# Stick-breaking attention: one hand-ordered pipeline over all head pairs, with each block's totals carried in one row of the next block

## The chip, the cores and the metric

The kernel runs on one core of one Trainium2 chip, as one program. The metric is the device time in microseconds (us) of one execution; the figure compared is the median over several executions. All durations in this document come from a profiled execution of the kernel or from its measured times.

## The reference

One layer of a hybrid decoder trunk, on 1024 positions of width 1024, in float32. `h` is the normalised input, and one wide projection gives the queries, keys and values of 8 heads of 64 columns, three conv operands and two gates:

```python
h = rms_norm(x, norm_mix_pre)
q, k, v, cb, cc, cx, g_att, g_conv = split(h @ w_in)
# per head and block of 128 queries, strictly causal (s < t):
z = q @ k.T / sqrt(64)
log_keep = where(strict, log_sigmoid(-z), 0)
later = reverse_cumsum(log_keep, axis=keys) - log_keep
w = where(strict, exp(log_sigmoid(z) + later), 0)
o = w @ v
y_att  = o @ w_att_branch
y_conv = (cb * causal_dwconv3(cc * cx)) @ w_conv_branch
m = sigmoid(g_att) * y_att + sigmoid(g_conv) * y_conv
x = x + rms_norm(m @ w_out, norm_mix_post)
h = rms_norm(x, norm_ffn_pre)
a, g = split(causal_dwconv3(h @ w_up))
x = x + rms_norm((gelu(g) * a) @ w_down, norm_ffn_post)
```

What matters here is `later`: for each query, the sum of softplus(z) = -log_keep over all keys that lie between a key and the query. A weight is exp(z - A), where A is the sum of softplus(z) over this key and all later ones.

## The kernel before

Every float32 operand of a large product is kept as two float16 parts, a high one (written by ScalarE, `AF.Copy`) and a low one (the rest, written by VectorE), and each product is three matrix passes (high-high, high-low, low-high; `PASSES`, `split` L84 to L87). A weight tile of 128x1024 is loaded, its sum of squares is taken on ScalarE (`sumsq`, L56), a one-column matmul and three small VectorE instructions give a power-of-two scale (`scale_of`, L74 to L79), and `split` makes the two halves. `wseq` is the order in which the weights are loaded, `prep` (and below it `wfetch`, `wsplit`) keeps a few of them ahead.

The layer runs in stages: the norm of x and its transposes with the v projection (in a hand order), the **attention stage** in `mixer`, then the branches, gates and output projection, then the feed-forward part.

The attention stage works on four head pairs `j`. For a pair the keys are cut into blocks `i` of 128 and the queries into halves `c` of 512. A **unit** is one key block against one query half, for both heads: keys on the 128 partitions, queries along the free dimension, so a tile is 128 x 2 x up to 512. Key blocks are taken from the last to the first; those on the diagonal have fewer queries (128, 256, 384 or 512). There are 12 units in a pair and 48 in all; 24 of them are 2x512 wide, and 8 each are 2x384, 2x256 and 2x128 wide. `attention(j)` writes each unit in four steps:

- `stage1`: scores into PSUM tile `z` (6 matmuls with 64 rows of weights, through `mm`, L600); VectorE scales them, bounds them at 44 and masks the diagonal block, into `zc` (L615 with a mask tile, L618 without); ScalarE takes exp and then ln(1 + .), giving `sp` = softplus (L622, L623); the halves of `sp` go into `sh` (L625 ScalarE, L626 VectorE).
- `stage2`: four matmuls with the triangle `tri[:, 0]` add, for each key, the sum over this and the later keys of the block into PSUM tile `A`, which lives for all units of a query half; VectorE forms `zc - A` (L638), ScalarE takes exp (L640), and the halves of the weights go into `w` (L642 ScalarE, L643 VectorE).
- `stage2b`: four matmuls more, with the complement of the triangle, `tri[:, 1]`, add the rest of the block's sum, so that every row of `A` holds the block's total when the next block comes:

```python
def stage2b(u):
    if u["i"] > 0:
        for h in range(2):
            for hl in range(2):
                mm(acc["A"][:, h, off:], self.tri[:, 1, :], sh[:, hl, h, off:], start=False, stop=False)
```

- `stage3`: six matmuls of the weights with `v16` into PSUM tile `o`; after the last block of a half ScalarE and VectorE write `o16` (L668, L669).

Between the units' steps, `merge` puts pieces of other work in proportion: the projections of the other head pairs (`qk_tile`), the v tiles, the conv operands and the gates (each 24 matmuls of 512 columns per half, `cm_half`, L200), and half of the conv branch's product (`branch(0, d, pm)`, L580, evicted by VectorE at L587). These need 3 of the 8 PSUM banks (`pm`); `z` and `A` have two each and `o` has one. The written order is not the final one: a scheduler orders the instructions of PE, DVE and ACT, with raised priority for the units.

SyncE's queue (SP) issues the weight loads in order. GpSimd (POOL) only makes masks at the start and does a few small powers.

Of the kernel before, what the change touches and what calls it, by code (L numbers as in the profile page):

```python
# [24 lines left out]
P = 128  # L25
T = 1024
# [5 lines left out]
EPS = 1e-6  # L32
GROUPS = (2, 4, 4, 4, 4, 4)
# [4 lines left out]
class Layer:  # L38
# [43 lines left out]
    nsc = 0  # L82

# [122 lines left out]
    def build(self):  # L206
# [7 lines left out]
        nt("q", 0), nt("k", 0)  # L214
        for j in range(4):
            if j < 3:
                nt("q", j + 1), nt("k", j + 1)
            nt("cc", j), nt("cx", j), nt("cb", j)
        nt("gc", 0), nt("ga", 0)
# [10 lines left out]
        with ExitStack() as top:  # L230
# [24 lines left out]
            self.tri = c.tile([P, 2, P], F16, tag="tri", name="tri")  # L255
            nc.vector.tensor_copy(self.tri[:, 0, :], tri32)
            nc.vector.tensor_scalar(self.tri[:, 1, :], tri32, -1.0, 1.0, ALU.mult, ALU.add)
# [6 lines left out]
    def mixer(self, mid):  # L264
        tc, nc, a = self.tc, self.nc, self.a
        hT = self.hp.tile([P, 2, KD, T], F16, tag="hT", name="hT")
        with ExitStack() as ph1:
# [12 lines left out]
            def qk_tile(j, which):  # L280
                w, inv = self.prep(f"{which}{j}") if j else self.wdone[f"{which}0"]
# [3 lines left out]
                s = stk[j]  # L285
                for c in range(2):
                    ps = pm.tile([P, NH], F32, tag="pm", name=f"p{which}{j}_{c}")
                    yield from self.cm_half(w[0], hT, ps, c)
                    sl = ds(c * NH, NH)
                    nc.scalar.activation(s[which][:, 0, sl], ps, AF.Copy, scale=2.0 ** -15)  # L290
                    nc.vector.scalar_tensor_tensor(s[which][:, 1, sl], ps, 2.0 ** -15, s[which][:, 0, sl],
                                                   ALU.mult, ALU.subtract)
                if which == "k":
                    cz = self.small(f"cz{j}", keep=True)
                    self.mul(cz[:, 0:1], s["iq"], inv)
                    self.mul(cz[:, 1:2], cz[:, 0:1], cst[:, 0:1])
                    s["cz"] = cz[:, 1:2]
                yield


            with tc.tile_pool(name="ptp", bufs=2, space=bass.MemoryType.PSUM) as ptp:
# [28 lines left out]

                def v_out(tt, pv):
                    pj = pv.rearrange("p (j two d) -> p j two d", two=2, d=64)
                    nc.scalar.activation(v16[tt // 2][:, tt % 2, :, 0:4:3, :], pj, AF.Copy, scale=2.0 ** -15)
                    for e in range(2):
                        nc.vector.scalar_tensor_tensor(v16[tt // 2][:, tt % 2, :, 1 + e, :], pj[:, :, e, :], 2.0 ** -15,
                                                       v16[tt // 2][:, tt % 2, :, 3 * e, :], ALU.mult, ALU.subtract)

                def v_tile(tt):
                    pv = pm.tile([P, NH], F32, tag="pm", name=f"pv{tt}")
# [8 lines left out]
                    v_out(tt, pv)  # L348
# [61 lines left out]
                with tc.manual_schedule(engines={ET.PE, ET.DVE, ET.Activation}):  # L410
# [78 lines left out]
                    gens0 = [qk_tile(0, "q"), qk_tile(0, "k")]  # L489
                    run(gens0[0], 8)  # L490
# [7 lines left out]
                    run(gens0[1], 8)  # L498
                    turn_x(7)
                    high(7)  # L500
                    low(7)

# [10 lines left out]
            def conv_tile(j):  # L513
                sm = self.small(f"cv{j}", keep=True)
                t = {}
                u = self.slot([P, T], F32, f"u{j}")
                for n, which in enumerate(("cc", "cx", "cb")):
                    w, inv = self.prep(f"{which}{j}")
                    self.mul(sm[:, n:n + 1], inv_h, inv)
                    sc = sm[:, n:n + 1]  # L520
                    if which == "cb":
                        pf[j] = self.slot([P, T], F32, f"pf{j}")
                        nc.scalar.activation(pf[j], u, AF.Copy, scale=self.cmw[:, j, 2:3])
                        for lag in (1, 2):
                            nc.vector.scalar_tensor_tensor(pf[j][:, lag:], u[:, :T - lag],
                                                           self.cmw[:, j, 2 - lag:3 - lag],
                                                           pf[j][:, lag:], ALU.mult, ALU.add)
                    for c in range(2):
                        ps = pm.tile([P, NH], F32, tag="pm", name=f"p{which}{j}_{c}")
                        yield from self.cm_half(w[0], hT, ps, c)  # L530
                        sl = ds(c * NH, NH)
                        if which == "cc":
                            nc.scalar.activation(u[:, sl], ps, AF.Copy, scale=sc)
                        elif which == "cx":
                            nc.vector.scalar_tensor_tensor(u[:, sl], ps, sc, u[:, sl], ALU.mult, ALU.mult)
                        else:
                            nc.vector.scalar_tensor_tensor(pf[j][:, sl], ps, sc, pf[j][:, sl],
                                                           ALU.mult, ALU.mult)
                self.sumsq(pf[j], smp_[:, j:j + 1], f"p{j}")
                yield  # L540

            def p_split():
                s_, inv = self.scale_of(smp_, 4, keep=True)
                acts[0] = []
                for j in range(4):
                    t = self.slot([P, 2, T], F16, f"p16_{j}")
                    self.split(t, pf[j], s_, f"p{j}")
                    acts[0].append(t)
                inv_x[0] = inv
                yield  # L550

            sig = {}

            def gate0(which):

                w, inv = self.prep(f"{which}0")
# [3 lines left out]
                for c in range(2):  # L560
                    ps = pm.tile([P, NH], F32, tag="pm", name=f"p{which}0_{c}")
                    yield from self.cm_half(w[0], hT, ps, c)
                    nc.scalar.activation(s[:, ds(c * NH, NH)], ps, AF.Copy, scale=sc)
                sig[which, 0] = s

            def branch(bi, d, pm):

                which = ("wc", "wa")[bi]
                w, inv = self.prep(f"{which}{d // 2}")
# [716 lines left out]
```

## Time and profile before

| what | value |
|---|---|
| time, median of 3 executions | 1369.34 us (1369.21 to 1369.62) |
| span of the profiled execution, first to last instruction | 1365.7 us |
| median less the span: what lies around the span | 3.6 us |
| TensorE (PE) busy | 1336.1 us (98%) |
| VectorE (DVE) busy | 1028.6 us (75%) |
| ScalarE (ACT) busy | 860.7 us (63%) |
| mean granted TensorE clock | 0.998 |

The profiled execution's own time is not listed apart from its span; the times in the table are those of the unprofiled executions. A PE that is busy is not a PE at its peak, since matmuls are pipelined: the mean duration of one 512-column matmul is 379 ns, but in a row they follow one another more closely, and the busy time of a group counts overlapped time once.

The stages in the trace: the v and first q, k halves until about 57 us; the attention stage with the work put between its units from there until 442 us, where the last matmul of `branch(0, 7, pm)` ends; branches, gates and output projection after that; the feed-forward part to the end.

### The profile page before, as it was taken

What the parts mean: (1) busy time and instruction counts of PE and PEld (TensorE: products, weight loads), DVE (VectorE), ACT (ScalarE), POOL (GpSimd) and SP (SyncE); (2) the same over time, 40 slices, a digit from 0 to 9 for tenths busy, and PEclk for the clock granted to TensorE, in tenths of its full rate; (3) what the DMA queues carried; (4) which work ended last, traced back from release to release, by engine and by line L of the source; (5) the groups of instructions that cost most, each with busy time, mean ns of one, the idle gap of its engine ahead of it and who ended that gap; (6) DMA issues with size and microseconds to landing.
All of it is one profiled execution on the core that took longest, in us unless ns stands there. A gap on an engine that the chain in (4) does not pass through costs nothing. (4 is left out here: it accounts for less than half of the span.)

```text
span 1365.7 us, 16990 instructions
## 1 busy us (share of the span) xinstructions
PE 1336.1 (98%) x6651; PEld 607.7 (44%) x6651; DVE 1028.6 (75%) x1610; ACT 860.7 (63%) x1204; POOL 34.2 (3%) x52
## 2 busy tenths in 40 slices
PE   6999999999999999999999999999999999999997
PEld 3444444444444444444454444444444444444443
DVE  6667777777775965878788985984894896699855
ACT  6668778787775775666466577652761673476524
POOL 2000000000000000000010000000000000000002
PEclk9999999999999999999999999999999999999999
DMA  7102111101111121351331123122220321313216
GB/s 264 62 1 62 32 31 32 38 25 39 40 31 47 32 62 31 93 185 36 119 124 62 62 62 123 39 87 85 70 78 16 123 62 62 109 45 124 63 46 109
DMA packets 26576, 96.06 MB, mean 70 GB/s; under 512 B 3072, under 2 KB 3200, under 8 KB 26496
## 3 DMA queue, kind: packets, MB, share of 16 engines
q1 hardware_dynamic: 25056, 89.74, 20.3%
q0 software_dynamic: 1440, 5.24, 2.1%
q8 instruction: 52, 0.85, 0.2%
q14 instruction: 28, 0.23, 0.1%
HBM read 86.58 MB, written 8.39 MB: 70 GB/s over the span
## 5 line engine op out<-in xcount | busy, mean ns | idle before, releaser
L1156 PEld LDWEIGHTS <-wh_u 128*128 128x128 f16 x1848 | 178.8, 98 | 217.3 <-issue 3.5
L1048 PE MATMUL pd<-wdh,f 128*128 128x512 f16 (+1 forms) x1068 | 230.3, 377 | 2.8 <-ACT wdh L86 1.2
L1048 PEld LDWEIGHTS <-f 128*128 128x128 f16 x1068 | 104.4, 98 | 127.2 <-issue 4.3
L86 ACT ACTIVATE wh_u<-ws_u,sc 128x1024 f16<-128x1024 f32 (+1 forms) x66 | 64.7, 998 | 102.9 <-DVE sc L78 79.3
L1055 DVE SCALAR_TENSOR_TENSOR yacc<-pd,sd,yacc 128x512 f32<-128x512 f32 (+1 forms) x81 | 58.5, 740 | 72.7 <-PE pd L1048 65.2
L1156 PEld LDWEIGHTS <-wh_g 128*128 128x128 f16 x588 | 56.9, 98 | 68.7 <-issue 0.4
L859 PE MATMUL py<-wh_wo,m 128*128 128x512 f16 x384 | 83.9, 379 | 0.0
L87 DVE SCALAR_TENSOR_TENSOR wh_u<-ws_u,sc,wh_u 128x1024 f16<-128x1024 f32 (+1 forms) x66 | 72.1, 1099 | 9.5 <-ACT wh_u L86 9.4
L643 DVE SCALAR_TENSOR_TENSOR w<-zc,w 128x1024 f16<-128x1024 f32 (+3 forms) x48 | 45.7, 955 | 34.5 <-ACT w L642 34.4
L622 ACT ACTIVATE sp<-zc 128x1024 f32<-128x1024 f32 (+3 forms) x48 | 40.2, 838 | 46.7 <-DVE zc L615 29.1
L600 PE MATMUL A<-sh,tri 128*128 128x512 f16 (+3 forms) x352 | 67.8, 322 | 0.0
L1233 DVE SCALAR_TENSOR_TENSOR ugu<-cgu,cw_g,ugu 128x1023 f32<-128x1023 f32 (+1 forms) x44 | 56.2, 1278 | 11.3 <-ACT ugu L1231 10.9
L1233 DVE SCALAR_TENSOR_TENSOR ua<-cau,cw_a,ua 128x1023 f32<-128x1023 f32 (+1 forms) x44 | 56.1, 1276 | 1.4 <-ACT ua L1231 1.3
L859 PEld LDWEIGHTS <-m 128*128 128x128 f16 x384 | 37.5, 98 | 44.1
L626 DVE TENSOR_TENSOR sh<-sp,sh 128x1024 f16<-128x1024 f32 (+3 forms) x48 | 45.7, 952 | 12.9 <-ACT sh L625 12.7
L640 ACT ACTIVATE zc<-zc 128x1024 f32<-128x1024 f32 (+3 forms) x48 | 40.0, 834 | 15.4 <-DVE zc L638 15.0
L638 DVE SCALAR_TENSOR_TENSOR zc<-A,zc 128x1024 f32<-128x1024 f32 (+3 forms) x48 | 45.5, 949 | 2.3 <-PE A L600 2.3
L56 ACT ACTIVATE jk_u<-ws_u 128x1024 bf16<-128x1024 f32 x44 | 46.4, 1054 | 0.9
L200 PE MATMUL pk<-hT,wh_k 128*128 128x512 f16 x192 | 46.8, 380 | 0.0
L200 PE MATMUL pq<-hT,wh_q 128*128 128x512 f16 x192 | 44.3, 379 | 1.3 <-DVE sc L79 1.3
L623 ACT ACTIVATE sp<-sp,one 128x1024 f32<-128x1024 f32 (+3 forms) x48 | 44.6, 928 | 0.8
L200 PE MATMUL pcb<-hT,wh_cb 128*128 128x512 f16 x192 | 44.8, 379 | 0.0
(620 smaller groups left out, 2606.4 us busy)
## 6 DMA issues: line engine op xcount, KB each, us to landing
ws_u<-w_up_nt SPq DMA_DIRECT2D x44, 512.0 KB, 3.7
ds<-w_down SPq DMA_DIRECT2D x22, 512.0 KB, 6.1
wd<-w_down SPq DMA_DIRECT2D x22, 512.0 KB, 3.7
ws_g<-w_in_nt SPq DMA_DIRECT2D x14, 512.0 KB, 3.6
x<-x SPq DMA_DIRECT2D x8, 512.0 KB, 8.0
ws_wo<-w_out SPq DMA_DIRECT2D x8, 512.0 KB, 7.1
xr<-x SPq DMA_DIRECT2D x8, 512.0 KB, 4.3
out<-x SPq DMA_DIRECT2D x7, 512.0 KB, 2.9
```

Source lines behind the costliest of these rows:

```text
L56: self.nc.scalar.activation(self.junk(f"jk_{name}"), src, AF.Square, accum_out=acc)
L86: self.nc.scalar.activation(dst[:, 0, :], src, AF.Copy, scale=s)
L87: self.nc.vector.scalar_tensor_tensor(dst[:, 1, :], src, s, dst[:, 0, :], ALU.mult, ALU.subtract)
L200: nc.tensor.matmul(ps, w[:, wi, ds(k * P, P)], hT[:, hi, k, ds(c * NH, NH)], start=n == 0, stop=n == last)
L600: nc.tensor.matmul(out, w, mv, skip_group_check=True, **kw)
L626: nc.vector.tensor_tensor(sh[:, 1, :, off:], sp[:, :, off:], sh[:, 0, :, off:], ALU.subtract)
L643: nc.vector.scalar_tensor_tensor(w[:, 1, :, off:], zc[:, :, off:], 2.0 ** 14, w[:, 0, :, off:], ALU.mult, ALU.subtract)
L859: nc.tensor.matmul(ps, m16[k][:, hi, ds(tt * P, P)], wo[k][:, wi, sl], start=k == 0 and p == 0, stop=k == 7 and p == 2)
L1048: nc.tensor.matmul(pd[nh], f16[g][k][:, hi, ds(tt * P, P)], w[k][:, wi, ds(*part)], start=run is runs[0] and n == 0, stop=run is runs[-1] ...
L1055: nc.vector.scalar_tensor_tensor(y[:, sl], ps, sm[:, 0:1], y[:, sl], ALU.mult, ALU.add)
L1156: nc.tensor.matmul(ps, w[wt][:, wi, ds(wc * NH + k * P, P)], self.block(i, hi, k), start=first and n == 0, stop=n == 3 * KH - 1, skip_grou ...
L1233: nc.vector.scalar_tensor_tensor(u[:, lag:], c[:, :T - lag], sm[:, 2 - lag:3 - lag], u[:, lag:], ALU.mult, ALU.add)
```

## The change

The attention stage is written anew:

- **Totals.** The complement matmuls (`stage2b`) and the second triangle are gone. `A` is a fresh tile for each unit (`sums`). Row 0 of `A` holds the sum over the whole block; `carry` adds this one row, by a VectorE instruction on one partition, to one row of the next block's `sp`. An operand may start at partition 96, so keys 96 and 127 of each block change places (`swap` for k: three small VectorE copies per key half; `swap_v` for v: rows through DRAM, 4 DMAs on SP's queue for each of the four `v16` tiles), and triangle and mask are made to match (small GpSimd instructions at the start).
- **Weights.** They are exp(z) times exp(-A) instead of exp(z - A). ScalarE reads the scores from PSUM itself (`expz`, with the scale as an operand), VectorE bounds e = exp(z) in SBUF at 1.2e19 (`bound`; the 128 diagonal columns with the mask, the others with one constant), ScalarE takes exp(-A) from PSUM (`expa`), VectorE multiplies (`times`).
- **Order.** PE, DVE and ACT run the whole stage in the written order (`manual_schedule`). One loop goes over all 48 units: `sums(k)`, `scores(k+2)`, side matmuls, `carry(k+1)` and so on. The side work on ACT and DVE (evictions, weight splits, conv taps) is queued in `Side` and let out at three places in each turn of the loop (`q.point`), by a budget per engine; a PSUM bank that is wanted and not yet evicted forces its eviction at that place.
- **Side work.** The order of weights is `FILL`, up to four ahead; the second halves of q0 and k0 move behind the start of the attention; the four halves `branch(0, 4..7)` are evicted by ScalarE, the sigmoid of the first gates comes at the end of the stage.

The core of the diff (the queued forms of the conv, gate and weight work are left out, they hold the same instructions as before; so are `p_ops` and `need`):

```diff
+EMAX = 1.2e19
+FILL = ("q0 k0 q1 k1 cc0 cx0 q2 k2 cb0 cc1 cx1 cb1 cc2 cx2 q3 k3 cb2 cc3 cx3 cb3 gc0 ga0").split()
...
-            self.clamp = att.tile([P, 2, NH], F16, tag="clamp", name="clamp")
-            nc.gpsimd.memset(self.clamp, 44.0)
-            nc.gpsimd.affine_select(self.clamp[:, :, :P], self.clamp[:, :, :P], [[0, 2], [1, P]], ALU.is_gt,
-                                    -30000.0, base=0, channel_multiplier=-1)
+            self.mask = att.tile([P, 2, P], F16, tag="mask", name="mask")
+            nc.gpsimd.memset(self.mask, 1.0)
+            nc.gpsimd.affine_select(self.mask, self.mask, [[0, 2], [1, P]], ALU.is_gt, 0.0, base=0,
+                                    channel_multiplier=-1)
+            nc.gpsimd.affine_select(self.mask[96:128, :, 97:], self.mask[96:128, :, 97:], [[0, 2], [0, 31]],
+                                    ALU.is_ge, 1.0, base=30, channel_multiplier=-1)
...
+            def swap_v(i):
+                rows = [dram.tile([1, 2, 4, 4, 64], F16, tag=f"vr{i}_{e}", name=f"vr{i}_{e}") for e in range(2)]
+                for e, r in enumerate((96, 127)):
+                    nc.sync.dma_start(rows[e], v16[i][r:r + 1])
+                for e, r in enumerate((127, 96)):
+                    nc.sync.dma_start(v16[i][r:r + 1], rows[e])
...
+                    kb = x.rearrange("p h (b t) -> p h b t", t=P)[:, :, 4 * c:4 * c + 4]
+                    kt = self.smp.tile([P, 2, 4, 1], F16, tag="kt", name=f"kt{j}{c}", bufs=2)
+                    nc.vector.tensor_copy(kt, kb[:, :, :, 96:97])
+                    nc.vector.tensor_copy(kb[:, :, :, 96:97], kb[:, :, :, 127:128])
+                    nc.vector.tensor_copy(kb[:, :, :, 127:128], kt)
...
+            def expz(u):
+                off = u["off"]
+                e = u["e"] = att.tile([P, 2, NH], F32, tag="e", name=f"e{u['nm']}", bufs=3)
+                nc.scalar.activation(e[:, :, off:], u["z"][:, :, off:], AF.Exp, scale=stk[u["j"]]["cz"])
+
+            def bound(u):
+                off, e = u["off"], u["e"]
+                if u["diag"]:
+                    dg = slice(off, off + P)
+                    nc.vector.scalar_tensor_tensor(e[:, :, dg], e[:, :, dg], EMAX, self.mask, ALU.min, ALU.mult)
+                    off += P
+                if off < NH:
+                    nc.vector.tensor_scalar(e[:, :, off:], e[:, :, off:], EMAX, None, ALU.min)
+
+            def softplus(u):
+                off = u["off"]
+                sp = u["sp"] = att.tile([P, 2, NH], F32, tag="sp", name=f"sp{u['nm']}", bufs=2)
+                nc.scalar.activation(sp[:, :, off:], u["e"][:, :, off:], AF.Ln, bias=self.one)
+
+            def carry(u):
+                if not u["top"]:
+                    A, o0 = acc["A"]
+                    nc.vector.tensor_tensor(u["sp"][96:97, :, o0:], A[0:1, :, o0:], u["sp"][96:97, :, o0:], ALU.add)
...
+            def sums(u):
+                off, sh = u["off"], u["sh"]
+                A = pat.tile([P, 2, NH], F32, tag="A", name=f"A{u['nm']}")
+                acc["A"] = A, off
+                for h in range(2):
+                    for hl in range(2):
+                        mm(A[:, h, off:], self.tri, sh[:, hl, h, off:], start=hl == 0, stop=hl == 1)
+
+            def expa(u):
+                off = u["off"]
+                g = u["g"] = att.tile([P, 2, NH], F32, tag="g", name=f"g{u['nm']}", bufs=1)
+                nc.scalar.activation(g[:, :, off:], acc["A"][0][:, :, off:], AF.Exp, scale=-1.0)
+
+            def times(u):
+                off, e = u["off"], u["e"]
+                nc.vector.tensor_tensor(e[:, :, off:], e[:, :, off:], u["g"][:, :, off:], ALU.mult)
...
-                def stage2b(u):
-                    if u["i"] > 0:
-                        off, sh = u["off"], u["sh"]
-                        for h in range(2):
-                            for hl in range(2):
-                                mm(acc["A"][:, h, off:], self.tri[:, 1, :], sh[:, hl, h, off:],
-                                   start=False, stop=False)
...
+            with tc.manual_schedule(engines={ET.PE, ET.DVE, ET.Activation}):
+                pump()
...
+                base = 18.0
+                for k in range(nu + 1):
+                    n = (est[k] * lam - att_pe[k]) / chunk
+                    at(sums, k)
+                    at(scores, k + 2)
+                    run_to(base + 0.35 * n)
+                    at(carry, k + 1)
+                    at(sp_high, k + 1)
+                    at(expa, k)
+                    if ready:
+                        ready.pop(0)[1]()
+                    q.point(free[k])
+                    at(sp_low, k + 1)
+                    at(expz, k + 2)
+                    at(times, k)
+                    at(bound, k + 2)
+                    at(w_high_, k)
+                    q.point(free[k])
+                    run_to(base + 0.65 * n)
+                    at(softplus, k + 2)
+                    at(w_low_, k)
+                    at(weigh, k - 1)
+                    q.point(free[k])
+                    run_to(base + n)
+                    if ready:
+                        ready[0][0]()
+                    base += n
+                run_to(total)
...
+    def bank(self, name):
+        while len(self.live) >= 3:
+            t = next(t for t in self.first + self.rest if any(o.bank == self.live[0] for o in t.ops))
+            self.late.append((name, self.live[0], len(t.ops)))
+            self.step(t)
+        self.live.append(name)
+        return self.tile(name)
...
+    def point(self, share=1.0):
+        self.clock += 1
+        for e in self.credit:
+            self.credit[e] = min(self.credit[e] + share, self.CAP)
+        for lst in (self.first, self.rest):
+            for t in list(lst):
+                self.advance(t)
+                if not t.ops and t in lst:
+                    lst.remove(t)
```

Of the loop's numbers, `n` is the count of side pieces (three matmuls each, 400 in all) put into turn `k`, `est[k]` a weight that grows with the widths of the units k to k+2, and `lam` scales these weights so that all pieces are used up at the end.

More of the change, by code (lines that the diff above doesn't have):

```diff
@@ L542, in p_split @@
[L542 to L556, printed above, removed]
+            sig = {}
+            wtasks, wpos = {}, [3]
@@ new lines, in mixer @@
+                q.drain("end")
+                for name, t in wtasks.items():
+                    if any(o.eng == "sum" for o in t.ops):
+                        for o in t.ops[:2]:
+                            if o.cost == 1.2:
+                                o.f()
+                        st = next(o.st for o in t.ops if o.st)
+                        self.wraw[name] = st["sm"], [st["t"]]
+                    else:
+                        q.force(t, name)
+                for which in ("gc", "ga"):
+                    nc.scalar.activation(sig[which, 0], sig[which, 0], AF.Sigmoid)
@@ L722, in mixer @@
+            self.fpos = wpos[0]
+            self.wpos = next((i for i, (n_, _) in enumerate(self.wseq) if i >= 3 and n_ not in self.wdone), n_w)
             pha.close()
```

592 lines of the change are left out of this document (413 added, 179 removed).

## The prediction

> **What bounds the kernel now.** First the page's busy times and slices, then a table of stretches, then the waits of PE.
>
> ```profile
> span 1365.7 us, 16990 instructions
> ...
> PE 1336.1 (98%) x6651; PEld 607.7 (44%) x6651; DVE 1028.6 (75%) x1610; ACT 860.7 (63%) x1204; POOL 34.2 (3%) x52
> ...
> PE   6999999999999999999999999999999999999997
> ```
>
> PE is busy in every slice but the first and the last. A busy PE need not be a full one, so the next view is the attention stage by itself, with three other stretches.
>
> ```profile
> core 0: us, PE busy (x) PEld busy (x) DVE busy (x) ACT busy (x) POOL busy (x), PEclk, DMA share, GB/s
> 57.30:442.30 385.00, 383.65 (x2154) 167.56 (x2154) 271.33 (x420) 285.98 (x379) 0.00 (x0) 1.00 0.12 36
> 442.30:475.00 32.70, 31.46 (x148) 14.35 (x148) 32.56 (x39) 25.01 (x37) 0.00 (x0) 1.00 0.11 33
> 700.00:780.00 80.00, 76.65 (x367) 35.76 (x366) 71.44 (x116) 46.13 (x73) 6.23 (x6) 1.00 0.20 66
> 1180.00:1260.00 80.00, 80.00 (x376) 36.28 (x375) 74.48 (x114) 54.36 (x74) 0.00 (x0) 1.00 0.29 102
> ```
>
> The first row is the stage that the change rewrites: 385.0 us, PE busy for 383.65 at full clock, ACT for 286 (74%), DVE for 271 (70%). The waits of PE from 40 to 560 us are these two, and no more:
>
> ```profile
> PE pr L74 <- DVE ywc L587: 1.3, 1, 1.3
> PE pq L200 <- DVE sc L79: 1.3, 1, 1.3
> ```
>
> So this stage is bound by PE's work: no unit's chain and no eviction is late in it. What leaves PE there shortens the stage, as long as ACT and DVE still deliver in time.
>
> **The sum of the change: PE.** What goes is `stage2b`. Each pair has three units of a half c=0 and seven of a half c=1 with i > 0: of these two are 128 columns wide, two 256, two 384 and four 512. With 4 matmuls per unit and 4 pairs that is 32 matmuls each of 128, 256 and 384 columns and 64 of 512. The rows of `A` hold them with the sums, which stay:
>
> ```profile
> L600 PE MATMUL A<-sh,tri 128*128 128x512 f16 x160 | 40.2, 379 | 0.0
> L600 PE MATMUL A<-sh,tri 128*128 128x384 f16 x64 | 13.6, 327 | 0.0
> L600 PE MATMUL A<-sh,tri 128*128 128x256 f16 x64 | 10.5, 274 | 0.0
> L600 PE MATMUL A<-sh,tri 128*128 128x128 f16 x64 | 6.8, 221 | 0.0
> ...
> 382.78 1.89 PE L600 MATMUL A<-sh,tri 128*128 128x512 f16 x8
> ```
>
> The complement's share is 64/160 of 40.2 and half of the other three: 16.1 + 6.8 + 5.25 + 3.4 = 31.5 us. That share counts the lead-in of each group. Eight in a row take 1.89 us (last row), the last one of them 0.379, so the other seven follow at 0.216 us, where the share gives 40.2/160 = 0.251. At that ratio the complement is 27.1 us. I take 29, with 27.1 and 31.5 as ends. Scores, sums, weighted sums, the 400 pieces of side work and the scale totals stay as many on PE as they were.
>
> **DVE.** It loses the scaling with the bound, from PSUM, and gets it back as `bound`; `zc - A` becomes `times`, the same size at the same price; new are `carry`, the swaps of k, and a lost eviction.
>
> ```profile
> L618 DVE TENSOR_SCALAR zc<-z,cz x16: 1271/1283/1285, 111.8 to 388.1; 128x1024 f32<-128x1024 f32 x16
> L615 DVE SCALAR_TENSOR_TENSOR zc<-z,cz,clamp x32: 474/878/1285, 64.5 to 355.9; 128x256 f32<-128x256 f32 x8, 128x512 f32<-128x512 f32 x8, 128x768 f32<-128x768 f32 x8, 128x1024 f32<-128x1024 f32 x8
> ...
> L638 DVE SCALAR_TENSOR_TENSOR zc<-A,zc 128x1024 f32<-128x1024 f32 x24 | 29.2, 1216 | 0.8 <-PE A L600 0.8
> L638 DVE SCALAR_TENSOR_TENSOR zc<-A,zc 128x768 f32<-128x768 f32 x8 | 7.6, 948 | 0.0
> L638 DVE SCALAR_TENSOR_TENSOR zc<-A,zc 128x512 f32<-128x512 f32 x8 | 5.5, 681 | 1.4 <-PE A L600 1.4
> L638 DVE SCALAR_TENSOR_TENSOR zc<-A,zc 128x256 f32<-128x256 f32 x8 | 3.3, 417 | 0.0
> ...
> L78 DVE TENSOR_SCALAR sc<-sc 128x1 int32<-128x1 int32 x26 | 3.8, 150 | 0.4
> ...
> 3.00 0.21 DVE L257 TENSOR_SCALAR tri<-tri 128x128 f16<-128x128 f32 x1
> ...
> L587 DVE TENSOR_SCALAR ywc<-pywc,sgn x8: 743/750/751, 424.5 to 442.7; 128x512 f32<-128x512 f32 x8
> ```
>
> - Removed: 16 x 1.28 + 32 x 0.878 = 48.6 us, and 8 x 0.750 = 6.0 us of branch evictions that go to ACT.
> - `carry`: its width is that of the unit before it, for 40 units: 16 of 1024 elements, 8 each of 768, 512 and 256. No row shows an instruction on one partition. Its ends are that it costs what a one-element instruction does (0.150 us, 6 us in all) and what the same elements cost on 128 partitions, as L638 does from the same PSUM tile: 16 x 1.216 + 8 x (0.948 + 0.681 + 0.417) = 35.8 us. I take 35.8, since in L638's rows the price follows the elements of a partition.
> - `bound`: the diagonal part, 256 elements with a mask, 32 x 0.474 = 15.2 us (L615's smallest). The rest has `carry`'s widths. At L638's rate it is 35.8 us; but L638 grows by (1216 - 417)/768 = 1.04 ns an element, and L257, float32 from SBUF with constants, took 0.21 us for 128, which after 0.150 leaves 0.5 ns. At that rate 1024, 768, 512 and 256 elements are 0.68, 0.55, 0.42 and 0.28 us, 20.9 us in all. I take 20.9, as L257 is the nearer row in kind.
> - Swaps of k: 21 copies at 0.150 is 3.1 us.
>
> DVE: 271.3 - 48.6 - 6.0 + 35.8 + 15.2 + 20.9 + 3.1 = 291.7 us, up to 306.6 with the slower `bound`. [...]
>
> ```profile
> 388.08 1.28 DVE L618 TENSOR_SCALAR zc<-z,cz 128x1024 f32<-128x1024 f32 x1
> 389.27 1.21 DVE L638 SCALAR_TENSOR_TENSOR zc<-A,zc 128x1024 f32<-128x1024 f32 x1
> ```
>
> These two overlap by 0.09 us. If `carry` and the instruction behind it each lose that, DVE has 40 x 0.18 = 7 us more, 314 at the worst. [...]
>
> **ACT.** Still five passes per unit.
>
> ```profile
> L622 ACT ACTIVATE sp<-zc 128x1024 f32<-128x1024 f32 x24 | 25.3, 1054 | 26.3 <-DVE zc L618 17.6 <-DVE zc L615 8.7
> L325 ACT ACTIVATE hT<-pt_pre,g_pre 128x1024 f16<-128x1024 f32 x8 | 8.8, 1106 | 8.0 <-PE pt_pre L322 8.0
> L585 ACT ACTIVATE ywc<-pywc,sgn x8: 667/687/689, 447.0 to 464.5; 128x512 f32<-128x512 f32 x8
> ```
>
> `expz` reads PSUM with a scale operand as L325 does, 0.05 us dearer than L622; over 36 units' worth of full width 1.9 us. The eight evictions from DVE are 5.5 us. ACT: 286.0 + 7.4 = 293.4.
>
> **What hides what.** With 29 us less the stage lasts 356. ACT then has 82% of it, DVE 82% (worst 88%). Two stretches of the feed-forward part, quoted above, show PE with DVE that full: at 93% PE lost nothing in 80 us, at 89% it lost 3.35. Their mean is 1.7 in 80, for 356 us 7.5, with 0 and 15 as ends. I add 7.5.
>
> The new recurrence, `sums` to `carry` to `sp_high` to `sp_low` to the next `sums`, is no bound by itself:
>
> ```profile
> L625 ACT ACTIVATE sh<-sp 128x1024 f16<-128x1024 f32 x24 | 25.0, 1043 | 0.6 <-PE A L600 0.6
> L626 DVE TENSOR_TENSOR sh<-sp,sh 128x1024 f16<-128x1024 f32 x24 | 29.2, 1216 | 1.3 <-ACT sh L625 1.3
> ```
>
> Four matmuls, 3 x 0.216 + 0.379 = 1.03, then 1.22, 1.04 and 1.22 us: 4.5 at full width, where 356/48 = 7.4 us pass per unit on average. But `carry` is a new wait on DVE for PE, and `sp_high` a new one on ACT for DVE; behind the first stand `sp_low`, `times` and the side work of the turn, behind the second `expa`, `expz` and `w_high_`. That is the first rival.
>
> Moves that I cost at nothing: the 16 row DMAs of `swap_v` stand in SP's queue ahead of the weights, which are fetched up to four ahead, with 48 side pieces of 3 x 0.216 = 0.65 us in front of the first that needs one, 31 us:
>
> ```profile
> ws_q<-w_in_nt SPq DMA_DIRECT2D x4, 512.0 KB, 3.9
> ```
>
> A row out and back is two DMAs in turn, by this row's landing 8 us, which the 31 cover; without that cover PE would wait for those 8 once. The masks are made at the start, where GpSimd's mask of 2x512 gets four times smaller. At the stage's start PE's wait at L200 (1.3 us) may go, since v6 comes first; the next that can be late there is the score tile of the first unit, which has 6 side pieces before it. The wait for `ywc` at L74 then is one for ACT. At its end the last unit still has `expa` to `o16`; the branch products in `wc` do not need it. That may cost 0 to 7 us; I take 1.3, and start and end cancel.
>
> Sum: -29 + 7.5 = -21.5 on the profile's span of 1365.7, 1344.2. The median of the runs, 1369.34, lies 3.6 above the span, so **1347.8 us**. This case's own range: -31.5 - 1.3 + 0 is 1336.5, -27.1 + 15 + 7 is 1364.2.
>
> **Rivals.**
>
> *1. In a fixed order ACT stands behind DVE, and DVE behind PE (slower).* In the written turn ACT's `sp_high(k+1)` waits for `sums(k)` and `carry(k+1)`, 1.0 + 1.22 us at full width, and `w_high_(k)` for `times(k)`, 1.22. Before, the scheduler put other work there: ACT's idle time of 385 - 286 = 99 us was free to lie anywhere. Over 24 full units and 24 of about 60%, the first wait is 24 x 2.2 + 24 x 1.3 = 84 us, the second the sum of L638's busy times, 45.6. Where side work of the turn before fills these gaps, nothing is lost; unfilled, ACT needs 293 + 130 = 423 us, and the stage lasts that. It is slower than before from 385 - 293 = 92 of 130 unfilled, 71%. At 80% the stage is 397, +12: 1381 us. For it: ACT and DVE are over 80% full, and side work is let out at three places only. Against: the next rows are two of the five passes over all 48 units.
>
> ```profile
> L622 ACT ACTIVATE sp<-zc 128x1024 f32<-128x1024 f32 (+3 forms) x48 | 40.2, 838 | 46.7 <-DVE zc L615 29.1
> L623 ACT ACTIVATE sp<-sp,one 128x1024 f32<-128x1024 f32 (+3 forms) x48 | 44.6, 928 | 0.8
> ```
>
> Four at 40.2 and one at 44.6 are 205 us, so some 88 of ACT's 293 are side work that can lie in the gaps, and `sums` has 7.4 - 4.5 = 2.9 us of slack in a turn.
>
> *2. The gain goes into evictions (no change).* Three PSUM banks take a half of 24 x 0.216 = 5.2 us each, and an eviction now needs one of the three places in a turn for ACT and the next for DVE, 7.4/3 = 2.5 us apart. Before, PE waited for one once:
>
> ```profile
> PEld L200 <- DVE k L291: 1.1, 1, 1.1
> ```
>
> Of the 400 pieces, eight to a half but for the branch, about 40 halves lie behind others; at 0.6 us each (an estimate: half of that 1.1) 24 us come back, which is 1371.8 us, and 1359.8 if only half of them are late; 1366 in the middle. For it: DVE is also full right after the stage (32.56 of 32.70 us), so nothing can be put off. Against: a bank that is wanted forces its eviction ahead of the rest.
>
> **How the numbers follow.** Forecast 58%, rival 1 24%, rival 2 18%. A measurement here tells about 0.2%, 2.7 us. The forecast's range is faster throughout; of rival 2 I count 10 points faster, 4 the same, 4 slower. Faster 0.68, same 0.04, slower 0.28. The range starts at 1337, the forecast's best end, which leaves out some 5%, and reaches to 1382, in the middle of rival 1, which leaves out some 12%.
>
> **What would show it.** Matmuls into `A` fall from 352 to 192, and the stage, read to the last matmul of `pywc` 7, ends near 421 instead of 442. PE's waits in it are below 15 us in all. `carry` at 1024 elements shows near 1.2 us, `bound` near 0.7. If PE waits on `sp_low`, or on score tiles behind `expz`, for over 30 us, rival 1 holds; if on evictions, rival 2. A `carry` of several us, or ACT over 330 us busy, would prove the sum wrong.

## The result and the profile after

The changed kernel takes 1352.99 us (median of 4) where the kernel before takes 1369.28 us: 16.3 us less, ratio 0.990 with a 95% interval of 0.9879 to 0.992. In a second series the same kernel came to 1354.53 against 1368.38 (0.9908, 0.989 to 0.9926). One execution of the changed kernel in each series took longer (1358.6 us) and is part of these medians and ratios; without it the first series has a median of 1352.85 us, 0.988 of the time before.

The page of the changed kernel, its span, the busy time of PE and PE's slices:

```profile
span 1351.2 us, 16781 instructions
...
PE 1311.1 (97%) x6491; PEld 589.9 (44%) x6491; DVE 1047.4 (78%) x1689; ACT 864.1 (64%) x1213; POOL 34.5 (3%) x58
...
PE   5999999999988999999999999999999999999997
```

PE lost 25 us of work and 160 instructions (192 matmuls into `A` in place of 352), and two slices, the twelfth and thirteenth, are no longer full: they are the end of the attention stage. The table of stretches has the stage up to the last matmul of `branch(0, 7)`, and the time right behind it:

```profile
57.30:425.70 368.40, 358.38 (x1988) 149.44 (x1987) 290.26 (x501) 283.95 (x382) 0.00 (x0) 1.00 0.12 37
425.70:460.00 34.30, 31.30 (x149) 14.10 (x146) 31.61 (x42) 31.21 (x45) 0.00 (x0) 1.00 0.15 46
```

The stage went from 385.0 to 368.4 us, 16.6 less: PE's busy time fell by 25.3, its idle time rose from 1.35 to 10.0. Behind the stage PE waits 3.0 us where it waited 1.3. That is 14.9 in all, and the spans differ by 14.5. The medians differ by 1.8 us more. The 3.6 us that the prediction puts around the span come from a median and the span of one profiled execution; in the later series, which list time and span of each single execution, the two differ by 1.6 to 1.9 us, once by 2.8. So the profiled execution of the kernel before seems to have been a faster one: its 1365.7 us and 1.8 make 1367.5, and the four executions of the kernel before in the first series lie between 1367.49 and 1369.62 us.

The waits of PE from 45 to 455 us:

```profile
PE pywc L1439 <- ACT ywc L765: 2.6, 1, 2.6
PE pr L76 <- DVE rb L73: 2.2, 1, 2.2
PE pr_p L1439 <- DVE rb_p L706: 1.8, 1, 1.8
PE pcc L1439 <- ACT u L664: 1.4, 1, 1.4
PE pga L211 <- ACT sgc L734: 1.3, 1, 1.3
PE pcb L211 <- DVE sc_cb L89: 0.8, 1, 0.8
PE pga L1439 <- ACT sga L734: 0.8, 1, 0.8
PE pywc L760 <- ACT ywc L765: 0.8, 1, 0.8
PE z L785 <- ACT e L804: 0.5, 1, 0.5
PE pcb L1439 <- DVE pf L667: 0.4, 1, 0.4
PE A L785 <- DVE sh L832: 0.2, 1, 0.2
```

Only the rows of `z` and `A`, 0.7 us together, are the attention's own chain. All others wait for side work: an eviction that has to free a PSUM bank (`ywc`, `u`, `sgc`, `sga`, `pf`), or the scale of a weight or of the conv product (`rb`, `rb_p`, `sc_cb`). In us these are 7.3 for evictions and 4.8 for scales.

The new instructions, by form:

```profile
L785 PE MATMUL A<-sh,tri 128*128 128x512 f16 x96 | 24.6, 379 | 0.0
L785 PE MATMUL A<-sh,tri 128*128 128x384 f16 x32 | 6.5, 326 | 0.0
L785 PE MATMUL A<-sh,tri 128*128 128x256 f16 x32 | 5.0, 272 | 0.2 <-DVE sh L832 0.2
L785 PE MATMUL A<-sh,tri 128*128 128x128 f16 x32 | 3.1, 219 | 0.0
...
L823 DVE TENSOR_TENSOR sp<-A,sp 1x1024 f32<-1x1024 f32 x16 | 19.5, 1218 | 8.1 <-PE A L785 7.8
L813 DVE TENSOR_SCALAR e<-e 128x1024 f32<-128x1024 f32 x16 | 11.1, 693 | 5.8 <-ACT e L804 5.6
L810 DVE SCALAR_TENSOR_TENSOR e<-e,mask 128x256 f32<-128x256 f32 x32 | 13.5, 421 | 5.5 <-ACT e L804 5.3
```

`carry` on one partition costs 1.218 us, as much as `zc - A` before on 128 (1.216); `bound` 0.693 us.

### The profile page after: what moved, and what is told of

It reads as the page before. It is cut to its first block, busy times and chain, and to the rows that moved or that the text cites. A ratio compares the mean times of both kernels' runs of the same rounds, so it can differ in the third digit from the quotient of the medians.

```text
span 1351.2 us, 16781 instructions
## 1 busy us (share of the span) xinstructions
PE 1311.1 (97%) x6491; PEld 589.9 (44%) x6491; DVE 1047.4 (78%) x1689; ACT 864.1 (64%) x1213; POOL 34.5 (3%) x58
## 5 line engine op out<-in xcount | busy, mean ns | idle before, releaser
L828 ACT ACTIVATE sh<-sp 128x1024 f16<-128x1024 f32 (+3 forms) x48 | 40.4, 842 | 52.3 <-DVE sp L823 51.9
L823 DVE TENSOR_TENSOR sp<-A,sp 1x1024 f32<-1x1024 f32 (+3 forms) x40 | 35.9, 897 | 26.3 <-PE A L785 21.8
L858 DVE SCALAR_TENSOR_TENSOR w<-e,w 128x1024 f16<-128x1024 f32 (+3 forms) x48 | 45.8, 954 | 10.1 <-ACT w L854 9.9
L854 ACT ACTIVATE w<-e 128x1024 f16<-128x1024 f32 (+3 forms) x48 | 40.4, 843 | 17.4 <-DVE e L849 16.5
L818 ACT ACTIVATE sp<-e,one 128x1024 f32<-128x1024 f32 (+3 forms) x48 | 44.4, 925 | 6.0 <-DVE e L813 3.1
L849 DVE TENSOR_TENSOR e<-e,g 128x1024 f32<-128x1024 f32 (+3 forms) x48 | 45.7, 953 | 2.1 <-ACT g L845 2.0
L804 ACT ACTIVATE e<-z,cz 128x1024 f32<-128x1024 f32 (+3 forms) x48 | 43.1, 897 | 3.6 <-PE z L785 3.6
L211 PE MATMUL pcc<-hT,wh_cc 128*128 128x512 f16 x192 | 45.1, 380 | 0.0
```

The source lines that it names most:

```text
L211: nc.tensor.matmul(ps, w[:, wi, ds(k * P, P)], hT[:, hi, k, ds(c * NH, NH)], start=n == 0, stop=n == last)
L849: nc.vector.tensor_tensor(e[:, :, off:], e[:, :, off:], u["g"][:, :, off:], ALU.mult)
L858: nc.vector.scalar_tensor_tensor(w[:, 1, :, off:], u["e"][:, :, off:], 2.0 ** 14, w[:, 0, :, off:], ALU.mult, ALU.subtract)
```

## The experiments

For a common yardstick the table of stretches is read from 57.3 us to the first matmul of `pywa`, so that each row holds the same work of PE but for the complement. The first two numbers are the length and PE's busy time, and their difference is PE's waiting; DVE's and ACT's busy times are the fourth and fifth. Before, then after:

```profile
57.30:464.30 407.00, 404.41 (x2252) 177.01 (x2252) 293.27 (x447) 301.12 (x400) 0.00 (x0) 1.00 0.12 37
```

```profile
57.30:449.90 392.60, 379.57 (x2088) 158.97 (x2087) 311.84 (x533) 305.37 (x412) 0.00 (x0) 1.00 0.13 38
```

PE works 24.8 us less and waits 13.0 us where it waited 2.6. Two questions: what are the 160 matmuls worth, and what made PE wait? Theory 1: side work is late because, in the written order, it stands behind `carry` and what waits for it. Theory 2: the waits belong to the end of the stage, where the branch evictions were given to ACT.

**e1, the old order without the complement.** `if u["i"] > 0:` in `stage2b` becomes `if False:`.

> The kernel before with the 160 complement matmuls left out (the later blocks then lack the rest of the sum, so this part of the computation is missing). It prices the removed PE work in the old order. If PE's work bounds the stage there and the complement costs what its rows' steady rate gives, 1369.3 falls by 25 to 29 us, to about 1342. If the complement was partly hidden or the order around it now becomes late on ACT or DVE, by 10 to 18 us only. After, which falls by 16.3, would be the whole effect of the matmuls if this shows 16.

1348.83 us against 1368.35, ratio 0.986 (0.9845 to 0.9874): 19.5 less. The row and PE's one new wait:

```profile
57.30:445.50 388.20, 381.98 (x2092) 161.57 (x2093) 291.79 (x447) 304.34 (x403) 0.00 (x0) 0.99 0.12 39
```

```profile
PE A L600 <- ACT sh L625: 4.4, 1, 4.4
```

Neither number was met. PE's work falls by 22.4 us, but this also holds work at a lower granted clock behind the 4.4 us wait: 0.79 and 0.87 in the two stretches of 10 us from 390 to 410 us, some 3 us by an estimate from these clocks. The scheduler's order of such a kernel is another order, so this is a lower bound for the price, not the price.

**e2, the matmuls put back into the new order.**

```diff
-                for h in range(2):
-                    for hl in range(2):
-                        mm(A[:, h, off:], self.tri, sh[:, hl, h, off:], start=hl == 0, stop=hl == 1)
+                for _ in range(2 if u["i"] > 0 else 1):
+                    for h in range(2):
+                        for hl in range(2):
+                            mm(A[:, h, off:], self.tri, sh[:, hl, h, off:], start=hl == 0, stop=hl == 1)
```

> The changed kernel with 160 matmuls of the complement's sizes put back: each block sum with i > 0 is made twice, the second overwriting the first. If PE is the bound of the stage also after the change, with some 10 us of waits at fixed places, the time rises by the whole price, 24 us, to 1377 (slower than before, by what the new waits cost). If the waits are slack of ACT and DVE, the longer turn covers them: PE's waits fall from 10 to 2 us and the time rises by 14 to 18 us, to 1369, the time of before.

1375.7 us, ratio to before 1.0055 (1.004 to 1.007): slower than before, and 22.7 us over the changed kernel, nearer to the first of the two expectations.

```profile
57.30:469.60 412.30, 403.22 (x2247) 173.04 (x2245) 311.65 (x533) 305.54 (x412) 0.00 (x0) 1.00 0.12 36
```

PE's work rises by 23.65 us, and of PE's waits the longer turns cover 4 (9.1 left of 13.0). So the matmuls are worth 23.65 us, 0.148 each, and the rest of the change costs: with the same PE work it is slower than before. The changed kernel's timeline gives nearly the same price. Four sums of one width in a row:

```profile
68.49 0.39 PE L785 MATMUL A<-sh,tri 128*128 128x128 f16 x4
74.61 0.60 PE L785 MATMUL A<-sh,tri 128*128 128x256 f16 x4
81.51 0.81 PE L785 MATMUL A<-sh,tri 128*128 128x384 f16 x4
115.40 1.03 PE L785 MATMUL A<-sh,tri 128*128 128x512 f16 x4
```

Less the mean of one (219, 272, 326 and 379 ns), each of the other three takes 0.057, 0.109, 0.161 and 0.217 us. For 32 matmuls each of the first three widths and 64 of the last that is 24.4 us.

**e3, without the carry,** and **e6, a carry of one query per head.** e3 leaves out the instruction of `carry`; e6 cuts its ranges to `o0:o0 + 1`.

> The changed kernel with carry left out (the totals of the later blocks are then missing). It takes 36 us from DVE and, from ACT, the wait of sp_high for it (51.9 us in the profile of after). Theory 1, evictions are late because ACT stands behind carry: PE's waits in the stage fall from 10 us to under 3, time 1346 or less. Theory 2, the waits come from the last pair alone, where the evictions of the branch product were given to ACT and where the conv weights' sums are chained: waits stay at 6 to 8 us, time 1350 to 1352.

> carry adds only the first query of each head (two elements in place of up to 1024, so all other totals are missing). The wait of sp_high for carry stays where it is, DVE's work falls by about 30 us (36 us less 40 times 0.15). Leaving carry out altogether took 9.2 us of PE's waits away. Theory 1a, the length of carry counts, in DVE's queue and in the way ACT must wait: PE's waits fall about as far as without carry, time 1345 to 1347. Theory 1b, the order counts, that ACT stands behind DVE and DVE behind sums at all: waits stay above 6 us, time 1350 to 1353.

e3: 1345.22 us, ratio 0.983 (0.9816 to 0.9845). e6: 1346.35 us, 8.2 under the changed kernel in the same series (**e5**, 1354.53), ratio 0.9842 (0.9827 to 0.9857). e5 was to set the level:

> The changed kernel unaltered, as the reference for the other runs of this call. Both theories expect what was measured first: 1353 us, 16 us under the kernel before.

The rows of e3 and of e6, then ACT's wait of `sp_high` for `carry` in the changed kernel and in e6:

```profile
57.30:440.70 383.40, 379.52 (x2091) 158.89 (x2090) 277.00 (x493) 307.41 (x413) 0.00 (x0) 1.00 0.12 38
```

```profile
57.30:443.60 386.30, 380.66 (x2088) 159.23 (x2087) 283.96 (x534) 305.79 (x413) 0.00 (x0) 1.00 0.13 39
```

```profile
L828 ACT ACTIVATE sh<-sp 128x1024 f16<-128x1024 f32 (+3 forms) x48 | 40.4, 842 | 52.3 <-DVE sp L823 51.9
```

```profile
L829 ACT ACTIVATE sh<-sp 128x1024 f16<-128x1024 f32 (+3 forms) x48 | 40.3, 841 | 41.0 <-DVE sp L823 40.7
```

PE's work stays; its waits fall from 13.0 to 3.9 and to 5.6 us. In e6 `sp_high` still waits for `carry` 40.7 us in all (51.9 in the changed kernel), so that an order with a wait in it is not what costs, but the length of the full `carry`, 28 us of DVE's time within the turns. Whether these 28 us cost as load on DVE, or by making late what stands behind `carry` in the turn, neither run can tell, since both shorten both.

**e7, more work for DVE away from the carry.** Behind `w_low_`, one instruction on one partition of a tile that nobody reads again:

```diff
+            def extra(u):
+                off, g = u["off"], u["g"]
+                nc.vector.tensor_tensor(g[96:97, :, off:], g[96:97, :, off:], g[96:97, :, off:], ALU.add)
...
                     at(w_low_, k)
+                    at(extra, k)
```

> The changed kernel with 46 us more work for DVE, away from the carry: one instruction on one partition per unit, on a tile that nobody reads again, behind w_low; the result stays right. If DVE's load alone makes the evictions late, DVE (82% full in the stage) comes to 95%, PE's waits rise by 10 us or more, time over 1362. If the load doesn't count but the wait in the chain from sums to sp_high does, the time stays within 3 us of the changed kernel.

1381.22 us, ratio 1.0096 (1.0081 to 1.0111): 26.7 over e5.

```profile
57.30:477.00 419.70, 388.39 (x2088) 160.84 (x2086) 359.54 (x581) 305.97 (x412) 0.00 (x0) 0.98 0.12 35
```

For 47.7 us more of DVE, PE waits 31.3 us (18.3 more), and the same matmuls keep it busy 8.8 us longer, with a granted clock of 0.98. So work of DVE that stands away from the carry costs too: 0.38 us of PE's waiting per us of DVE here, where e6 gives back 0.27 (7.4 for 27.9); in time it is 0.56 and 0.29. But this is no clean price of load. The new instruction also makes the next `carry` late:

```profile
L828 ACT ACTIVATE sh<-sp 128x1024 f16<-128x1024 f32 (+3 forms) x48 | 40.4, 842 | 70.7 <-DVE sp L823 70.4
```

And `g` has one buffer, so that the next `expa` now waits for the new instruction, 4.6 us in all. DVE is busy for 359.5 of 419.7 us only; of the other 60, some 48 are waits for a step of ACT or PE in the same turn (`sp_low` for `sp_high` 14.9, `bound` for `expz` 11.1, `w_low_` for `w_high_` 10.0, `carry` for `sums` 7.5, the rest 4.2), in which the written order lets nothing else run on DVE.

**e8, the branch evictions back on DVE.** The `Op("A", 0.6, ...)` of `branch` becomes `Op("V", 0.7, ...)` with `nc.vector.tensor_scalar`.

> The changed kernel with the eight evictions of the branch product given back to DVE (as before the change). Theory 2, the move of these to ACT makes the waits at the end of the stage (2.6 and 0.8 us for ywc in the profile of after): these two go, time 1349 to 1350. Theory 1, whichever engine evicts stands in the same queue order: the waits change places, time within 1.5 us of the changed kernel.

1355.21 us, 0.7 over e5: no gain. PE's waits for `ywc` change from ACT to DVE (2.3 and 1.4 us). So the evictions on ACT are not the cause. The other half of theory 2, the place, is right in good part: 9.4 of the changed kernel's 13.0 us of waits lie behind 350 us (PE is busy for 90.5 of the last 99.9 us), and of the 3.9 us left in e3 all but 0.1.

**e4 and e11, another order on ACT.**

```diff
+                    at(expa, k)
                     at(carry, k + 1)
+                    at(expz, k + 2)
                     at(sp_high, k + 1)
-                    at(expa, k)
...
-                    at(sp_low, k + 1)
-                    at(expz, k + 2)
                     at(times, k)
+                    at(sp_low, k + 1)
                     at(bound, k + 2)
```

> The changed kernel with the order within a turn changed: ScalarE runs expa(k) and expz(k+2) ahead of sp_high(k+1), VectorE runs times(k) ahead of sp_low(k+1). Nothing else. ScalarE then has work while VectorE runs carry. Theory 1: ACT's wait of sp_high for carry falls from 51.9 to under 15 us, PE's waits from 10 to 3 or 4, time 1346 to 1348. Theory 2: ACT's wait falls as much, but PE's waits stay at 8 to 10 and the time within 1 us of 1353. If the longer way from sums to the next sums (carry now comes after expa, 1.0 us later, and sp_low after times, 1.2 us later) is over the 2.9 us of slack, PE waits on sp_low and the time rises over 1355.

> e4 unaltered, as the reference of this call and to set it against the changed kernel. If e4's gain of 1 to 3 us is real, the ratio to the kernel before is 0.987 again and its interval lies below 0.990; if not, it comes to 0.990 as the changed kernel's.

1351.0 us (ratio 0.9872, 0.9856 to 0.9889) and, again, 1352.78 (0.9881, 0.9865 to 0.9898); both intervals reach into the changed kernel's. The second interval does end below 0.990, as was asked, but the changed kernel's own 0.988 of above lies in it too, so this tells nothing. PE's waits fall from 13.0 to 9.5 us in both runs, while PE is busy 1.2 and 3.1 us longer. If the order gains, it is 2 us at most. What moved is in e4's groups, the idle time behind the last bar:

```profile
L828 ACT ACTIVATE sh<-sp 128x1024 f16<-128x1024 f32 (+3 forms) x48 | 40.4, 842 | 10.5 <-DVE sp L823 10.5
L823 DVE TENSOR_TENSOR sp<-A,sp 1x1024 f32<-1x1024 f32 (+3 forms) x40 | 35.9, 897 | 56.9 <-ACT g L845 56.6
```

ACT waits for `carry` 10.5 us in place of 51.9, but `carry` now waits 56.6 us for `expa`. It reads nothing that `expa` writes; both read the PSUM tile `A`, and `carry` waits for `expa` 34 times, 3.9 us at the longest; in the five turns from 109 to 146 us it starts 0.03 to 0.04 us after the end of `expa`, the reader ahead of it. What makes it wait was not shown. The wait changed its owner.

**e9 and e10, work from DVE to GpSimd,** on e4's order: in e9 the copies of `swap` and the casts of the weight sums, in e10 also `bound` of the 16 full off-diagonal units (`nc.vector` becomes `nc.gpsimd`).

> The order of e4 (expa and expz ahead of sp_high, times ahead of sp_low), and the small copies that DVE makes for the key swap (24 at 0.17 to 0.19 us) and for the weight sums (some 23 casts at 0.15) are given to GpSimd, which does nothing in the stage. DVE loses 8 us of 290. If DVE's time is the price, at the 0.27 to 0.58 us per us of DVE that e6 and e7 show, the time falls by 2 to 4 us against e4: 1347 to 1349. If GpSimd's copies come later than DVE's did, keys and scales are late for PE: 1352 or more.

> As e9, and the bound of the 16 full off-diagonal units is given to GpSimd, 11 us less for DVE. By the same price another 3 to 6 us: 1343 to 1346. Against it: GpSimd is on the way from expz to softplus; an instruction of 1024 elements that takes 2 us or more there, or slows DVE beside it, makes softplus late by more than is won: 1352 to 1365.

e9: 1351.99 us (0.9877, 0.9862 to 0.9891), 0.8 under e11, too little to tell. In its stretch DVE is busy for 6.6 us less than in e11 (302.95 for 309.59), and PE's waits stay at 9.5 us: not every us of DVE has the price that was expected from e6 and e7.

e10: 1353.95 us (0.9897, 0.9882 to 0.9911), a little worse. The rows of e9 and e10, then e10's row of the new instruction:

```profile
57.30:446.80 389.50, 380.04 (x2089) 158.61 (x2088) 302.95 (x483) 307.74 (x413) 22.65 (x48) 1.00 0.13 38
```

```profile
57.30:450.60 393.30, 382.20 (x2091) 159.15 (x2089) 302.63 (x467) 307.67 (x413) 68.17 (x64) 1.00 0.12 37
```

```profile
L814 POOL TENSOR_SCALAR e<-e 128x1024 f32<-128x1024 f32 x16 | 47.8, 2985 | 75.8 <-ACT e L804 70.9 <-PE pcx L211 4.9
```

2.99 us in place of 0.693, on the way from `expz` to `softplus`; but ACT waits for it only twice, 0.7 us in all. What went wrong is on DVE. It lost 11 us of `bound` and is busy as long as in e9 (302.6 us for 303.0), because others of its instructions became longer beside GpSimd: the low halves of the weight splits 39.2 us for 35.8, `times` 49.0 for 45.7, `sp_low` 47.7 for 45.7. Hardly any of DVE's time was saved.

**e12, the wait behind the stage.** On e9, the weights of the conv branch's product are split at most three ahead:

```diff
-                w, inv = self.wdone[f"{which}{d // 2}"] if later else self.prep(f"{which}{d // 2}")
+                w, inv = self.wdone[f"{which}{d // 2}"] if later else self.prep(f"{which}{d // 2}", 3 if bi == 0 else None)
+                if bi == 0 and not later:
+                    idx = [i for i, (n, _) in enumerate(self.wseq) if n == f"wc{d // 2}"][0]
+                    self.fetch_to(self.reach(idx, self.wahead + self.wlead))
```

> As e9, and behind the stage the weights are split at most three ahead while the rest of the conv branch's product runs, so that the one-column sum of the weight tile wa2, for which PE waits 2.2 to 2.3 us there (its cast stands behind ACT's sum of squares), comes after the next two products. If that wait is simply removed, the time falls by 2.2 us against e9's 1352.0, a little more where the wait of e11 also cost granted clock (24 matmuls took 6.95 us behind it in place of 5.34): 1348 to 1350. If the next instruction of PE waits for the same queue of ACT and DVE anyway, 1351 to 1353.

1348.5 us against 1366.71, ratio 0.9862 (0.9846 to 0.9879): 18.2 less than before, the fastest complete version; the interval ends where the changed kernel's begins. In this series the kernel before was 2.0 us faster than in e9's, so of the 3.5 us under e9 some 2 are left by the ratios.

```profile
57.30:445.20 387.90, 380.70 (x2093) 158.98 (x2091) 301.28 (x478) 307.52 (x412) 21.55 (x48) 1.00 0.12 37
```

PE's waits are 7.2 us; the 2.2 us for `rb` are gone and no other wait took their place.

## Why the prediction was right, step by step

The measured time, 1352.99, lies 5.2 over the 1347.8 forecast; the gain is 16.3 us for 21.5. Part of this nearness is luck: the sum held 3.6 us around the span, where the executions show 1.6 to 1.9. The spans themselves, 1351.2 for 1344.2, are 7.0 apart: 3.7 of it is PE's work (25.3 less for 29), 1.2 the waits in the stage, 1.7 those behind it.

- **PE bounds the stage, and the complement's matmuls leave it: right; their price was too high.** 29 was taken between 27.1 and 31.5; e2 measures 23.65, under the lower end. The rows' shares count the lead-in of each group, which the sums still pay when the complement behind them goes. The correction, 0.216 for 0.251, was taken from the 512-column form and applied to the narrow ones, where the lead-in weighs more: 0.39 us for four matmuls of 128 columns, of which three take 0.17. The lower bound should have been made form by form from start to start, 24.4 us.
- **DVE: right within 1%.** 291.7 us were worked out for the stage, 290.26 measured: `carry` 1.218 (1.216), `bound` 0.693 (0.68), the diagonal part 0.421 (0.474).
- **ACT:** 283.95 for 293.4. The sum was made against the old stage, which held the sigmoids (3.4 us with their table load of 1.28) and more of the last weight sums; nothing hung on it.
- **PE waits 7.5 more: near, and in part by luck.** 8.7 more in the stage. The term came from how full DVE is in two other stretches, of which the fuller one, 93%, cost nothing and the other, 89%, 3.35 us; so they did not show that fullness sets the waits. e3 and e6 show that the length of `carry` makes 7 to 9 us of them, and e9, on e4's order, that 6.6 us less of DVE elsewhere changed none. That work on DVE was the right thing to price is borne out; the size is a mean of two cases that came out well.
- **Start and end cancel: nearly.** The wait for `q` at the start is gone (1.3); behind the stage 1.7 came on top, but not from the last unit's tail that was priced: it is the 2.2 us for `rb`, a weight's scale.
- **Rival 1** (ACT behind DVE, slower) has its waits: `sp_high` 51.9 us and `w_high_` 16.5 of the 130 priced, but they lie within ACT's slack. PE waited 0.7 us for the attention's chain. e4 takes most of the first wait from ACT, puts as long a one on DVE, and gains at most 2 us.
- **Rival 2** (evictions late) names most of the waits that came: 7.3 us for evictions, in place of the 24 priced. Another 4.8 us are for scales, which it does not name. Its price rested on one wait of 1.1 us, and that one was listed for the weight load (PEld), not for PE.
- **The overlap that `carry` and the instruction behind it may lose** is lost. Five rows of DVE's timeline in the changed kernel (start, length):

```profile
397.63 0.15 DVE L101 TENSOR_TENSOR sgn<-sp,sc_wc 128x1 f32<-128x1 f32 x1
397.80 1.22 DVE L823 TENSOR_TENSOR sp<-A,sp 1x1024 f32<-1x1024 f32 x1
399.05 1.28 DVE L608 SCALAR_TENSOR_TENSOR wh_wc<-ws_wc,sc_wc,wh_wc 128x1024 f16<-128x1024 f32 x1
...
400.32 1.22 DVE L832 TENSOR_TENSOR sh<-sp,sh 128x1024 f16<-128x1024 f32 x1
401.45 1.22 DVE L849 TENSOR_TENSOR e<-e,g 128x1024 f32<-128x1024 f32 x1
```

The last two overlap by 0.09 us. `carry` (row two) starts 0.02 after the end of its forerunner, and the next 0.03 after `carry`'s end. In the whole stage 25 instructions right behind a `carry` have no wait listed, and all of them start 0.02 to 0.04 us after its end; of the 17 `carry` with no wait listed, 16 start 0.02 to 0.04 us after the end of their forerunner and one 0.13. The cause was not shown. Set against the 0.09 us of the last two rows, the loss is an estimated 0.1 us on each side, small beside the 1.22 us of the instruction itself.

Open: why DVE's time costs PE when it is busy for only 79 to 86% of the stretch was not taken apart. The runs show that `carry`'s length costs, that more work behind `w_low_` costs, and that less work in the small copies gains nothing clear; how much is load and how much delay within the turn stays open. No run let evictions out at more places in a turn.

## What to carry to other kernels

When an edit takes work from the bound engine and gives work to another in a fixed order, price both: here 23.7 us left PE, and the 36 us that DVE got for `carry` cost 7 to 9 of them back, though DVE was four fifths busy. An instruction on one partition was as dear here as on 128 (1.218 us and 1.216), so totals in a row were cheap in code and not in time. Where the waits of the bound engine went to side work, moving that work to another engine of the same queue order (e8, waits of 2.3 and 1.4 us) or turning the order round (e4, 51.9 us on ACT for 56.6 on DVE) changed the name of the wait; starting it where nothing waits for it (e12) removed one of 2.2 us. Moving 11 us of `bound` from DVE to GpSimd (e10) saved hardly any of DVE's time (302.6 us for 303.0): other instructions on DVE took 8.7 us more there than in e9.

## What the hardware showed that was not expected

Behind a PE wait of 2.2 us the granted clock fell in two runs, and not in others. The same place in e11 and in e4, the 24 matmuls behind the wait:

```profile
432.35 0.16 PE L76 MATMUL pr<-rb,ones 128*128 128x1 bf16 x1 [2.23 <-DVE rb L73]
432.37 6.95 PE L760 MATMUL pywc<-p,wh_wc 128*128 128x512 f16 x24
```

```profile
432.05 0.16 PE L76 MATMUL pr<-rb,ones 128*128 128x1 bf16 x1 [2.23 <-DVE rb L73]
432.08 5.34 PE L760 MATMUL pywc<-p,wh_wc 128*128 128x512 f16 x24
```

6.95 us for 5.34, 1.6 us more. In e11 the granted clock was 0.72 in the 5 us around the end of the wait and 0.56 from 433 to 436 us; in e4 it was 1.00 there. Nine profiled runs have a wait for `rb` at this place, of 1.6 us in e8 and of 2.2 to 2.3 us in the others. The clock fell behind it in e11 and e6 (again 6.95 us, with 0.54 from 427 to 430 us), and not in the other seven. What decides between the two was not shown.

GpSimd's small copies were dear. Of e9's three copies of 8 elements for the key swap the first took 0.807 us in the mean (0.19 to 1.12), the two right behind it 0.24 and 0.28; DVE's in the changed kernel took 0.166, 0.189 and 0.188. The first copy in e9, then in the changed kernel:

```profile
L338 POOL COPY kt<-k 128x8 f16<-128x8 f16 x8 | 6.5, 807 | 59.3 <-DVE k L327 46.9 <-DVE cz L101 12.4
```

```profile
L338 DVE COPY kt<-k 128x8 f16<-128x8 f16 x8 | 1.3, 166 | 0.1
```
